# Twelve gate tiles as six pairs of seven half-size products, in a one-core hybrid decoder step

## The chip, the cores and the metric

The kernel runs on one NeuronCore of a Trainium2 chip. The metric is device time of one launch in microseconds (us), median of the runs. TensorE multiplies (PE in the profile, PEld for its weight loads), VectorE (DVE), ScalarE (ACT) and GpSimd (POOL) do elementwise work, SyncE (SP) issues most of the DMAs, ACT's queue issues the weight loads.

## The reference, cut to what matters

One layer for 1024 prompt tokens and 8 sample tokens (1032 columns in all), width 1024, float32.

```python
h = rmsnorm(x, norm_g)
proj = h @ w_in                      # 1024 -> 7688 columns
(aq, ak, av, abeta, aalpha, agate, bu, bv, bgate, cq, cgate, mg) = split(proj)
ya = delta_branch(...)               # 4 heads: conv, SiLU, gated delta rule in chunks
yb = chunk_mlp_branch(bu, bv, bgate) # LayerNorm, causal 128x128 mixing per group
yc = memory_branch(cq, cgate, k, v)  # attention to 256 memory tokens
gates = sigmoid(mg + b_gate)         # 3 x 1024 columns of proj: 24 tiles of 128
merged = gates[0]*(ya @ w_br_a) + gates[1]*(yb @ w_br_b) + gates[2]*(yc @ w_br_c)
y = rmsnorm(x + merged @ w_out, final_norm_g)
```

The changed part computes half of `mg`: twelve of its 24 feature tiles.

## The kernel before, in words

Everything is kept transposed: features on partitions, tokens along the free dimension. `hTh` and `hTl` hold h, split into a high part (fp32r) and the rest, as 8 k-tiles of 128 x 1032. A weight tile of 128 output features is split the same way into `whi` and `wlo`. `mm3` makes one product as three passes (high x high, high x low, low x high) over the 8 k-tiles: 24 matmuls. A job ("k", "v", "q", "ag", "bv", "bg", "bu", "gate", "cq", "cg") is one weight tile: `project` runs `h_group` for NS = 3 token groups of NW = 344, so 72 matmuls on line L275, into the PSUM tag `pj` (2 buffers). Other PSUM tags are `tp` (2) and `dl` (4).

The program is written as one main stream of such jobs, with side streams (Python generators) mixed in by hand. `mm3` calls `tick()` after every sixth matmul; each side stream then issues its next piece; a piece that yields n sits out n ticks. No scheduler reorders anything: each engine takes its instructions in the order in which they were issued. `run.until(cond)` ticks without main matmuls between, until the condition holds.

The main stream has these parts:

- `norm_gen`: h is normed and transposed, while the first two weight tiles (k0, v0) run in four token groups of 256 or 264.
- `plan_a`: the jobs of the four delta heads, of branch B, and 8 gates (1 beside head 1, 7 at the end). The side stream `delta_all` starts after q0. For each head `delta_gen` issues transposes, `LA` (L784/L785), a way through DRAM (`ld` L795, `Lt` L799), a solve on POOL in 31 steps (`X`, L838/L844), a second way through DRAM (`ud` L850, `U` L852), three DVE transposes into `TA` and `T2` (L855 to L857), small products (L863 to L894), and a loop over 8 chunks (L902 to L920) that carries the state `S`. It ends with `ro`, `r` (L931) and the transposes of `r`. Beside it runs `sample_gen`. At the end of the plan stands `run.until(("delta", 3) in done)`.
- `plan_c`: two gates, then eight times a gate and a `kv` job (24 matmuls of 256 columns), then for each head cq, a gate, cg, and one more gate. Side streams: `mem_norm`, `b_gen` (branch B), `att_gen` (prompt attention) and `csample_all`, which runs `csample_gen` for the heads one after another: loads of the caches, `qd` and `qb` through DRAM (L1177, L1179), two multiplies on POOL (L1184), reduction, softmax, products L1215. It ends with `run.until({("att", 3), "b"} <= done)`.
- `plan_m`: gate 0 and the 24 branch products with the merge; then the output projection.

A gate tile is copied to a `stg` buffer (3 of them), passed through a sigmoid by `gate_spill`, and stored to DRAM until `merge` needs it. `w_next` loads weights two and three jobs ahead (on ACT's queue) and splits them one job ahead (ACT L250, DVE L253).

Of the kernel before, what the change touches and what calls it, by code (L numbers as in the profile page):

```python
# [118 lines left out]
def tile_mixer_step(ctx: ExitStack, tc: tile.TileContext, a):  # L119
# [124 lines left out]
    def w_split(i, slow=True, eng=V):  # L244
        if i < len(order) and i not in splits:
# [4 lines left out]
            S.copy(out=hi, in_=raws[i])  # L250
# [2 lines left out]
            eng.tensor_tensor(out=lo, in0=raws[i], in1=f32(hi), op=ALU.subtract)  # L253
# [18 lines left out]
    def mm3(out, wh, wl, rh, rl, nk, ticks=True):  # L272
        ops = [(w(k), r(k)) for w, r in ((wh, rh), (wh, rl), (wl, rh)) for k in range(nk)]
        for i, (w, r) in enumerate(ops):
            PE.matmul(out, lhsT=w, rhs=r, start=(i == 0), stop=(i == len(ops) - 1))  # L275
# [80 lines left out]
    xst = ExitStack()
    xp = scoped(xst, "xp")
    scT = xp.tile([P, 12, 24], F32, name="scT")
    wab = xp.tile([P, KT, 8], F32, name="wab")
# [593 lines left out]

    def gate_tile(i, t):
        br, f = gate_col[i]
        b = c_bg + br * 8 + f
        project("gate", i, lambda n, sl, o: S.copy(out=t[:, sl], in_=o))  # L957
        return dict(out=t, in_=t, func=AF.Sigmoid, bias=colv[:, b:b + 1])

    def gate_spill(i, t, act):  # L960
        yield 2
        S.activation(**act)
        gate_d[i] = dr.tile([P, NT], F32, name=f"gate{i}")
        SP.dma_start(out=gate_d[i], in_=t)
# [545 lines left out]
```

## Time and profile before

| | |
|---|---|
| Runs | 1150.77, 1152.01, 1152.36 us; median 1152.01 |
| Profiled execution | span 1148.6 us, granted TensorE clock 0.995 |
| Share of the span with work | PE 97%, PEld 94%, DVE 53%, ACT 36%, POOL 19% |
| DMA | 133.5 MB, 116 GB/s mean |
| Chain that ended last | PE 90%, of which line L275 into `pj` 56% and into `dl` 20% |

The span is the time from the first to the last instruction; the median of the runs lies 3.4 us above it. PE has work all the time but for the start. What matters in such a program is whether PE's next instruction has what it needs when its turn comes; the idle time of the other engines does not count by itself.

### The profile page before, as it was taken

The page shows a single profiled execution, that of the slowest core. Times are in us where ns is not written, and L with a number is a line of the kernel's source. Part 1 is how long each engine was busy: PE and PEld are TensorE (multiplying, and loading weights), DVE is VectorE, ACT ScalarE, POOL GpSimd, SP SyncE. Part 2 cuts the span into 40 slices and gives each one's busy share as a digit, 9 for nine tenths or more (in the row PEclk, how much of TensorE's full clock was granted, in tenths as well). Part 3 has the DMA queues.
Part 4 walks back from the last instruction along what each step waited for, and adds up shares of the span by engine and source line. Part 5 has one row for each costly group of instructions (what it writes and reads, how often), then busy time and mean ns, then how long its engine had stood idle before and what let it go on. Part 6 is the DMA issues. An engine that isn't in the chain of part 4 may idle for free.

```text
span 1148.6 us, 19257 instructions
## 1 busy us (share of the span) xinstructions
PE 1119.7 (97%) x7609; PEld 1074.8 (94%) x7609; DVE 609.7 (53%) x1512; ACT 411.9 (36%) x891; POOL 214.1 (19%) x392
## 2 busy tenths in 40 slices
PE   5999999999999999999999999999999999999997
PEld 4989999999999999999999999989999999998884
DVE  6754654655465546513277432655545246786554
ACT  5434233333331333333344333545445321232232
POOL 1060715070507050600034000101101000000000
PEclk9999999999999999999999999999999999999999
DMA  8104420341143114422654556543432465662221
GB/s 250 39 20 97 132 63 23 117 129 46 40 125 104 45 41 126 124 79 77 200 138 137 166 170 186 159 118 93 146 114 74 145 195 176 212 213 100 83 93 57
DMA packets 153772, 133.53 MB, mean 116 GB/s; under 512 B 20941, under 2 KB 134922, under 8 KB 153674
## 3 DMA queue, kind: packets, MB, share of 16 engines
q1 hardware_dynamic: 72242, 89.82, 24.5%
q10 hardware_dynamic: 81440, 42.49, 13.7%
q8 instruction: 60, 0.98, 0.3%
q14 instruction: 30, 0.25, 0.1%
HBM read 100.74 MB, written 31.64 MB: 115 GB/s over the span
## 4 chain that ended last, share of the span: by engine, by line
PE 90%; DVE 4%; DMA 2%; ACT 2%; issue 1%; SPq 1%; ACTq 0%; DVEq 0%
PE pj L275 56%; PE dl L275 20%; PE tp L191 2%; PE dl L191 2%; PE dl L784 1%; DMA raw<-w_in 1%; DMA stg<-ya 1%; PE dl L894 1%; PE tp L1094 1%; PE dl L918 1%; PE dl L909 1%; PE dl L902 1%; PE dl L904 1%; PE dl L917 1%; DVE wlo L253 1%
## 5 line engine op out<-in xcount | busy, mean ns | idle before, releaser
L275 PE MATMUL pj<-hTh,whi 128*128 128x344 f32 (+1 forms) x1456 | 280.7, 327 | 3.1 <-DVE ql L155 1.1
L275 PE MATMUL pj<-hTh,wlo 128*128 128x344 f32 (+1 forms) x1456 | 277.5, 325 | 0.0
L275 PE MATMUL pj<-hTl,whi 128*128 128x344 f32 (+1 forms) x1456 | 272.3, 322 | 0.0
L275 PEld LDWEIGHTS pj<-hTh,whi 128*128 128x128 f32 x1456 | 232.4, 190 | 5.9 <-ACT hTh L393 1.5
L275 PEld LDWEIGHTS pj<-hTh,wlo 128*128 128x128 f32 x1456 | 235.1, 189 | 1.4 <-issue 0.8
L275 PEld LDWEIGHTS pj<-hTl,whi 128*128 128x128 f32 x1456 | 234.3, 188 | 1.1 <-DVE hTl L394 0.2
L253 DVE TENSOR_TENSOR wlo<-raw,whi 128x1024 fp32r<-128x1024 f32 (+1 forms) x91 | 102.5, 1126 | 51.7 <-ACT whi L250 44.2
L250 ACT CAST whi<-raw 128x1024 fp32r<-128x1024 f32 (+1 forms) x92 | 86.2, 937 | 81.5 <-PE dl L275 64.8
L957 ACT COPY stg<-pj 128x344 f32<-128x344 f32 x72 | 32.1, 446 | 108.0 <-PE pj L275 107.6
L838 POOL TENSOR_TENSOR itmp<-X,Lt 128x60 f32<-128x60 f32 (+24 forms) x124 | 43.7, 352 | 125.7 <-DMA Lt<-ld 116.5
L1184 POOL TENSOR_TENSOR kvt<-kvt,qb 128x1024 f32<-128x1024 f32 x8 | 19.2, 2419 | 210.7 <-DMA qb<-qd 130.9
L275 PE MATMUL dl<-yh,whi 128*128 128x344 f32 x288 | 57.3, 321 | 0.0
L275 PE MATMUL dl<-yh,wlo 128*128 128x344 f32 x288 | 57.3, 321 | 0.0
L275 PE MATMUL dl<-yl,whi 128*128 128x344 f32 x288 | 57.1, 320 | 0.0
L275 PEld LDWEIGHTS dl<-yh,whi 128*128 128x128 f32 x288 | 47.8, 188 | 0.0
L275 PEld LDWEIGHTS dl<-yh,wlo 128*128 128x128 f32 x288 | 47.7, 188 | 0.0
L275 PEld LDWEIGHTS dl<-yl,whi 128*128 128x128 f32 x288 | 47.6, 188 | 0.0
L844 POOL TENSOR_TENSOR X<-X,itmp 128x60 f32<-128x60 f32 (+24 forms) x124 | 43.7, 353 | 9.7
L531 ACT COPY xraw<-pj 128x344 f32<-128x344 f32 (+2 forms) x38 | 16.3, 430 | 66.4 <-PE pj L275 63.1
L906 DVE COPY y<-dl 128x128 f32<-128x128 f32 x32 | 9.3, 291 | 55.3 <-PE dl L904 34.4
L1367 DVE TENSOR_TENSOR stg<-dl,stg 128x344 f32<-128x344 f32 x48 | 24.7, 515 | 18.1 <-PE dl L275 18.1
L503 POOL TENSOR_TENSOR kq<-kq,cvt 128x512 f32<-128x512 f32 x24 | 32.6, 1358 | 1.9
(378 smaller groups left out, 1591.9 us busy)
## 6 DMA issues: line engine op xcount, KB each, us to landing
raw<-w_in ACTq DMA_DIRECT2D x57, 512.0 KB
gate<-stg SPq DMA_DIRECT2D x23, 516.0 KB
stg<-gate SPq DMA_DIRECT2D x23, 516.0 KB
x<-x_prompt SPq DMA_DIRECT2D x8, 512.0 KB
raw<-w_mem_kv ACTq DMA_DIRECT2D x8, 512.0 KB
kvt<-cache_mem_k SPq DMA_DIRECT2D x16, 256.0 KB
kvt<-cache_mem_v SPq DMA_DIRECT2D x16, 256.0 KB
wor<-w_out SPq DMA_DIRECT2D x8, 512.0 KB
```

What stands on the lines that cost most here:

```text
L191: PE.transpose(out, in_, ident[:p, :p])
L250: S.copy(out=hi, in_=raws[i])
L253: eng.tensor_tensor(out=lo, in0=raws[i], in1=f32(hi), op=ALU.subtract)
L275: PE.matmul(out, lhsT=w, rhs=r, start=(i == 0), stop=(i == len(ops) - 1))
L503: G.tensor_tensor(out=d[:, cs], in0=d[:, cs], in1=o, op=ALU.add)
L531: S.copy(out=raw[:, 3 + sl.start:3 + sl.stop], in_=o)
L784: PE.matmul(t, lhsT=kq[:, 0, sl], rhs=kq[:, :, sl], start=True, stop=True)
L838: G.tensor_tensor(out=tm, in0=X[:, 0:m, j:j + 1].to_broadcast([P, m, n]), in1=Lt[:, j:j + 1, j + 1:32].to_broadcast([P, m, n]), op=ALU.mult,)
L844: G.tensor_tensor(out=X[:, 0:m, j + 1:32], in0=X[:, 0:m, j + 1:32], in1=tm, op=ALU.subtract)
L957: project("gate", i, lambda n, sl, o: S.copy(out=t[:, sl], in_=o))
L1184: G.tensor_tensor(out=kts[hb], in0=kts[hb], in1=qb[:, hb * 4:hb * 4 + 4].unsqueeze(2).to_broadcast([P, 4, 2, P]), op=ALU.mult,)
L1367: V.tensor_tensor(out=sg[:, sl], in0=o, in1=sg[:, sl], op=ALU.mult)
```

## The change

Gates 1 to 5 run first (1 and 2 while h is being normed, in the place of k0 and v0). Then gates 6 to 17 run in six pairs by Strassen's method in Winograd's form. For two weight tiles (two block rows) and h cut in two halves of 4 k-tiles and two halves of HT = 516 tokens, seven half products replace eight: each has 4 k-tiles, three passes and two column halves of QT = 258, so 24 matmuls, 168 for a pair. Sums of h blocks (`t_hl`, made by `t_gen`) and of weight blocks (`sf`, made on POOL by `pair_sums`) are operands; the results are added from PSUM by DVE. After that come the jobs of `plan_a` without any gates, and `plan_c` with 6 gates in place of 15. From the end of the pairs on, `tick()` is called after every fourth matmul (`run.every = 4`), and a yield of n sits out n * 6 / 4 ticks, rounded up. A bare yield still waits for one tick.

```diff
 class Streams:
...
     def __init__(self):
         self.items = []
+        self.every = 6
...
-                it[1] = next(it[0]) or 0
+                it[1] = -(-(next(it[0]) or 0) * 6 // self.every)
...
-    plan_a = [
-        [("k", 0), ("v", 0), ("q", 0), ("ag", 0), ("bv", 0), ("bv", 1), ("bv", 2)],
-        [("k", 1), ("v", 1), ("q", 1), ("ag", 1), ("bv", 3), ("bg", 0), ("bu", 0)] + gates(1),
-        [("k", 2), ("v", 2), ("q", 2), ("ag", 2), ("bg", 1), ("bu", 1), ("bg", 2), ("bu", 2)],
-        [("k", 3), ("v", 3), ("q", 3), ("ag", 3), ("bg", 3), ("bu", 3)] + gates(7),
-    ]
+    plan_0 = gates(5)
+    plan_s = gates(12)
+    plan_a = []
+    for h in range(H):
+        plan_a += [("k", h), ("v", h), ("q", h), ("ag", h)]
+        plan_a += ([("bv", 0), ("bv", 1), ("bv", 2)], [("bv", 3), ("bg", 0), ("bu", 0)],
+                   [("bg", 1), ("bu", 1), ("bg", 2), ("bu", 2)], [("bg", 3), ("bu", 3)])[h]
     plan_c = gates(2)
-    for j in range(8):
-        plan_c += gates(1) + [("kv", j)]
+    for j in range(0, 8, 2):
+        plan_c += [("kv", j), ("kv", j + 1)] + (gates(1) if j < 6 else [])
     n_kv = len(plan_c)
     for h in range(H):
-        plan_c += [("cq", h)] + gates(1) + [("cg", h)]
+        plan_c += [("cq", h), ("cg", h)]
     plan_c += gates(1)
...
-            if ticks and i % 6 == 5:
+            if ticks and i % run.every == run.every - 1:
                 tick()
...
+    def t_gen():
...
+        def minus(o, x, y, lo):
+            V.tensor_tensor(out=o, in0=f32(x[0]), in1=f32(y[0]), op=ALU.subtract)
+            G.tensor_tensor(out=lo, in0=f32(x[1]), in1=f32(y[1]), op=ALU.subtract)
...
+        f1, d, f2 = new(), new(), new()
+        minus(f1, h_blk(1, 2), h_blk(1, 1), d)
+        yield 5
+        V.tensor_tensor(out=f1, in0=f1, in1=d, op=ALU.add)
...
+        f3, d = new(), new()
+        minus(f3, h_blk(2, 2), h_blk(1, 2), d)
+        V.tensor_tensor(out=t_hl[4][1], in0=f4, in1=f32(t_hl[4][0]), op=ALU.subtract)
+        yield 5
+        V.tensor_tensor(out=f3, in0=f3, in1=d, op=ALU.add)
+        yield 2
+        S.copy(out=t_hl[3][0], in_=f3)
+        yield 2
+        V.tensor_tensor(out=t_hl[3][1], in0=f3, in1=f32(t_hl[3][0]), op=ALU.subtract)
+        done.add("tsum")
...
+    run.add(t_gen())
+    for _, i in plan_0[2:]:
+        t = stage()
+        run.add(gate_spill(i, t, gate_tile(i, t)))
+    run.until(lambda: "tsum" in done)
...
+    def product(banks, n, x, first):
+        wh, wl = wt[n]
+        for q in range(2):
+            ts = slice(q * QT, (q + 1) * QT)
+            ops = [(w, r, k) for w, r in ((wh, x[0]), (wh, x[1]), (wl, x[0])) for k in range(HK)]
+            for i, (w, r, k) in enumerate(ops):
+                PE.matmul(
+                    banks[q], lhsT=w[:, k], rhs=r[:, k, ts], start=(first and i == 0), stop=(i == len(ops) - 1),
+                    skip_group_check=True,
+                )
+                if i % run.every == run.every - 1:
+                    tick()
...
+    def pair_job(p, i, j):
...
+        pair_split(p, ("a12", 3))
+        b_a = bank(pj)
+        product(b_a, "a11", h_blk(1, 1), True)
+        for q in range(2):
+            S.copy(out=p1[:, qs[q]], in_=b_a[q])
+        pair_split(p, (4,))
+        b_b = bank(dl)
+        product(b_b, 2, t_hl[2], True)
+        plus(u2, b_b, p1)
...
+        product(b_b, 3, t_hl[3], False)
+        plus(u3, b_b, p1)
+        pair_sums(p + 2, (3, 4))
...
+        product(b_c, 4, h_blk(2, 2), False)
+        plus(ti[:, HT:], b_c, u2)
+        run.add(pair_store(i, j, ti, tj))
...
+    run.every = 4
...
+    for kind in ("k", "v", "q"):
+        project(kind, 0, qkv_tile(kind, 0))
```

Three places show what moves. On PE at the end of delta head 3, before (L275 is the main stream, L909 to L918 the last chunk, `ident,r` the last transposes of the head):

```order
L275 MATMUL pj<-hTh,wlo 128x344 x6
L909 MATMUL dl<-y,kd 128x128
L917 MATMUL dl<-S,gcb 128x128
L918 MATMUL dl<-y,LA 128x128
L275 MATMUL pj<-hTh,whi 128x344 x8
L275 MATMUL pj<-hTl,whi 128x344 x8
L275 MATMUL pj<-hTh,wlo 128x344 x8
L275 MATMUL pj<-hTh,whi 128x344 x8
L275 MATMUL pj<-hTl,whi 128x344 x4
L191 MATMUL dl<-ident,r 128x128 x4
```

Main matmuls stand between the steps of the head. After (the main stream is now L280, the same steps are L1121 to L1130, and `ident,r` ends the head):

```order
L1121 MATMUL dl<-y,kd 128x128
L1129 MATMUL dl<-S,gcb 128x128
L1130 MATMUL dl<-y,LA 128x128
L1114 MATMUL dl<-r,U 128x128
L1116 MATMUL dl<-S,Kg 128x128
L1121 MATMUL dl<-y,kd 128x128
L1129 MATMUL dl<-S,gcb 128x128
L1130 MATMUL dl<-y,LA 128x128
L195 MATMUL dl<-ident,r 128x128 x8
L280 MATMUL pj<-hTh,whi 128x344 x8
```

None stands there any more. The stretch without them begins on PE where the last job of `plan_a` ends (`kqn,st` to `dd` are `sample_gen`'s, L1075 and L1076 the first small products after `TA` and `T2`):

```order
L280 MATMUL pj<-hTh,wlo 128x344 x4
L195 MATMUL dl<-ident,kq 128x128 x4
L280 MATMUL pj<-hTh,wlo 128x344 x4
L898 MATMUL tp<-kqn,st 128x2 x8
L912 MATMUL tp<-do_7069,ones 128x8
L195 MATMUL tp<-ident,dd 8x128
L1075 MATMUL dl<-TA,LA 32x32
L1076 MATMUL dl<-T_7207,LA 32x32
```

From the last `LA` product of head 3 (L996, before L784) to L1075 there are 44 main matmuls now, for the other heads 240, before 294 for each. On PE at the end of `plan_c`, before (`pb`, `pTs` and `so` are steps of `csample_gen` for head 3):

```order
L191 MATMUL tp<-ident,pb 128x8 x2
L275 MATMUL pj<-hTh,whi 128x344 x6
L191 MATMUL tp<-ident,p 128x128 x2
L275 MATMUL pj<-hTh,whi 128x344 x2
L275 MATMUL pj<-hTl,whi 128x344 x8
L275 MATMUL pj<-hTh,wlo 128x344 x2
L1215 MATMUL tp<-kvt,pTs 32x128 x8
L275 MATMUL pj<-hTh,wlo 128x344 x6
L1215 MATMUL tp<-kvt,pTs 32x128 x8
```

After (the first three rows of L195 and L1415 are still head 2's, from `qsm` on it is head 3):

```order
L195 MATMUL tp<-ident,pb 128x8 x2
L1415 MATMUL tp<-kvt,pTs 32x128 x16
L195 MATMUL tp<-ident,so 128x128 x2
L195 MATMUL tp<-ident,qsm 8x128
L195 MATMUL tp<-ident,sc 8x128 x2
L195 MATMUL tp<-ident,pb 128x8 x2
L1415 MATMUL tp<-kvt,pTs 32x128 x16
L195 MATMUL tp<-ident,so 128x128 x2
L280 MATMUL pj<-hTh,whi 128x344 x8
```

The whole sample attention of head 3 now stands behind the last job of the plan, with nothing between its steps.

More of the change, by code (lines that the diff above doesn't have):

```diff
@@ L29 @@
 NS = 3
+HK = KT // 2
+HT = NT // 2
+QT = HT // 2
 H = 4
@@ L233, in w_of @@
         return w_in_v[:, :, c:c + P], KT
-    order = [(k, i) + w_of(k, i) for k, i in sum(plan_a, []) + plan_c + plan_m]
+    order = [(k, i) + w_of(k, i) for k, i in plan_0 + plan_s + plan_a + plan_c + plan_m]
+    in_pair = range(len(plan_0), len(plan_0) + len(plan_s))
     raws, splits, w_pos = {}, {}, [0]
@@ L244, in w_split @@
     def w_split(i, slow=True, eng=V):
-        if i < len(order) and i not in splits:
+        if i < len(order) and i not in splits and i not in in_pair:
             nk = order[i][3]
@@ L355, in tile_mixer_step @@
     SP.dma_start(out=a["sc_sample"][:, 0:2, :], in_=a["state_conv"][:, 1:3, :])
[L356 to L359, printed above, removed]
+    scT = const.tile([P, 12, 24], F32, name="scT")
+    wab2 = const.tile([P, KT, 16], F32R, name="wab2")
+    wab = np_.tile([P, KT, 8], F32, name="wab", bufs=1)
     SP.dma_start(out=wab, in_=w_in_v[:, :, O_AB:O_AB + 8])
-    wab2 = xp.tile([P, KT, 16], F32R, name="wab2")
     nss = np_.tile([P, 9], F32, name="nss", bufs=1)
@@ L399, in const_gen @@
         V.tensor_copy(out=colv, in_=t[:, :89])
+        done.add("const")
         yield
@@ L535, in qkv_tile, with gate_tile, gate_act, gate_store @@
         return evac
-    e_k, e_v = qkv_tile("k", 0), qkv_tile("v", 0)
+    def gate_tile(i, t):
+        br, f = gate_col[i]
+        b = c_bg + br * 8 + f
+        project("gate", i, lambda n, sl, o: S.copy(out=t[:, sl], in_=o))
+        return dict(out=t, in_=t, func=AF.Sigmoid, bias=colv[:, b:b + 1])
+    def gate_act(i):
+        br, f = gate_col[i]
+        b = c_bg + br * 8 + f
+        return dict(func=AF.Sigmoid, bias=colv[:, b:b + 1])
+    def gate_store(i, t):
+        gate_d[i] = dr.tile([P, NT], F32, name=f"gate{i}")
+        SP.dma_start(out=gate_d[i], in_=t)
+    def gate_spill(i, t, act):
+        yield 2
+        while "const" not in done:
+            yield
+        S.activation(**act)
+        gate_store(i, t)
     w_pos[0] = 2
     w2 = [splits.pop(0), splits.pop(1)]
+    t2 = [stage(), stage()]
     for n in range(4):
@@ L542, in tile_mixer_step @@
         sl = slice(n * 256, (n + 1) * 256 if n < 3 else NT)
-        for w, ev in zip(w2, (e_k, e_v)):
-            ev(NS - 1 if n == 3 else 0, *h_group(w, n, sl))
+        for w, t in zip(w2, t2):
+            _, o = h_group(w, n, sl)
+            S.copy(out=t[:, sl], in_=o)
             if n == 3:
@@ L547, in tile_mixer_step, with h_blk @@
                     pass
+    for i, t in zip((1, 2), t2):
+        run.add(gate_spill(i, t, dict(out=t, in_=t, **gate_act(i))))
+    run.until(lambda: "const" in done)
     nst.close()
-    project("q", 0, qkv_tile("q", 0))
+    sst = ExitStack()
+    tpl = scoped(sst, "tsum", side="right")
+    t_hl = {n: [tpl.tile([P, HK, HT], F32R, name=f"t{n}{x}") for x in "hl"] for n in (2, 3, 1, 4)}
+    def h_blk(i, j):
+        ks, ts = slice((i - 1) * HK, i * HK), slice((j - 1) * HT, j * HT)
+        return hTh[:, ks, ts], hTl[:, ks, ts]
@@ new lines, in tile_mixer_step, with pair_sums @@
+    run.add(t_gen())
[3 more added lines that the diff above has]
+    run.until(lambda: "tsum" in done)
+    tst.close()
+    spool = scoped(sst, "pair")
+    sf, s4, wt = {}, {}, {}
+    def pair_sums(p, which):
+        if p not in pairs:
+            return
+        a1, a2 = raws[p], raws[p + 1]
+        for n in which:
+            sf[n] = spool.tile([P, HK, P], F32, tag=f"sf{n}", name=f"sf{n}")
+            x, y, op = {
+                1: lambda: (a2[:, :HK], a2[:, HK:], ALU.add),
+                2: lambda: (sf[1], a1[:, :HK], ALU.subtract),
+                3: lambda: (a1[:, :HK], a2[:, :HK], ALU.subtract),
+                4: lambda: (a1[:, HK:], sf[2], ALU.subtract),
+            }[n]()
+            G.tensor_tensor(out=sf[n], in0=x, in1=y, op=op)
@@ new lines, in pair_split @@
+    def pair_split(p, names):
+        if p not in pairs:
+            return
+        a1, a2 = raws[p], raws[p + 1]
+        src = {"a11": a1[:, :HK], "a12": a1[:, HK:], "a22": a2[:, HK:]}
+        if len(names) == 1:
+            hi = spool.tile([P, HK, P], F32R, tag="s4h", name="s4h")
+            lo = spool.tile([P, HK, P], F32R, tag="s4l", name="s4l")
+        else:
+            hi = wp.tile([P, KT, P], F32R, tag="whi", name="whi")
+            lo = wp.tile([P, KT, P], F32R, tag="wlo", name="wlo")
+        for q, n in enumerate(names):
+            x = src[n] if n in src else sf[n]
+            h, l = hi[:, q * HK:(q + 1) * HK], lo[:, q * HK:(q + 1) * HK]
+            S.copy(out=h, in_=x)
+            V.tensor_tensor(out=l, in0=x, in1=f32(h), op=ALU.subtract)
+            wt[n] = (h, l)
@@ L551, in tile_mixer_step @@
+    pairs = list(in_pair)[::2]
+    w_load(pairs[0])
+    w_load(pairs[0] + 1)
+    pair_sums(pairs[0], (1, 2, 3, 4))
+    w_load(pairs[0] + 2)
+    w_load(pairs[0] + 3)
+    pair_split(pairs[0], ("a11", 2))
+    for p in pairs:
+        pair_job(p, order[p][1], order[p + 1][1])
+    w_pos[0] = pairs[-1] + 2
+    sst.close()
+    run.every = 4
+    xst = ExitStack()
+    xp = scoped(xst, "xp")
+    for kind in ("k", "v", "q"):
+        project(kind, 0, qkv_tile(kind, 0))
     dp = scoped(dst, "dp")
@@ L952, in delta_all @@
             yield from delta_gen(h)
[L954 to L964, printed above, removed]
     ug_t = {}
@@ L991, in tile_mixer_step @@
     run.add(delta_all())
-    for kind, i in sum(plan_a, [])[3:]:
+    for kind, i in plan_a[3:]:
         job(kind, i)
```

57 lines of the change are left out of this document (added).

## The prediction

> **What bounds the kernel now.** I read the page's busy shares first, then the busy time by stretch, and the timeline where the change moves something. The first row is the page's on PE; the second is a stretch with a delta head beside the main stream: us from and to, length, then PE, PEld, DVE, ACT and POOL busy with counts, granted clock, DMA share and GB/s.
>
> ```profile
> PE 1119.7 (97%) x7609; PEld 1074.8 (94%) x7609; DVE 609.7 (53%) x1512; ACT 411.9 (36%) x891; POOL 214.1 (19%) x392
> 165.00:279.00 114.00, 113.57 (x837) 111.15 (x837) 62.15 (x168) 40.13 (x104) 38.26 (x85) 1.00 0.29 84
> ```
>
> PE is covered even there. So time is the sum of PE's work, and two things can change it: what a matmul costs, and whether PE must now wait for a side stream.
>
> **The products.** Start-to-start distances of matmul groups give the price. These are PE rows: start, length, line, shapes, count.
>
> ```profile
> 30.88 1.11 PE L275 MATMUL pj<-hTh,whi 128*128 128x256 f32 x8
> 31.83 0.65 PE L275 MATMUL pj<-hTl,whi 128*128 128x256 f32 x4
> ...
> 684.25 1.44 PE L275 MATMUL pj<-hTl,whi 128*128 128x344 f32 x8
> 685.52 1.44 PE L275 MATMUL pj<-hTh,wlo 128*128 128x344 f32 x8
> 686.80 1.07 PE L275 MATMUL pj<-memTh,whi 128*128 128x256 f32 x8
> 687.71 1.07 PE L275 MATMUL pj<-memTl,whi 128*128 128x256 f32 x8
> ```
>
> A 344-column matmul takes 1.27/8 = 158.8 ns, one of 256 takes 0.95/8 = 118.8 on h and 0.91/8 = 113.8 on the memory tokens. For 258 I take 119.0, since most operands are h (119.7 if it grows with the columns). A pair cost 144 x 158.8 = 22.86 us and will cost 168 x 119.0 = 19.99: over six pairs -17.2 us (-22.5 at 113.8, -16.5 at 119.7).
>
> Here a rule of the Trainium skill speaks against the change: "Perfetto Trace Analysis", section "Identifying the Most-Contended Engine", counts weight-load busy time as the good measure for TensorE, and PEld stands at 94%. By that rule 24 more weight loads in a pair would cost, not save: 26.7 us a pair at 158.8 ns each, 1264 in all. The trace does not bear it out: the 256-column rows have a weight load for each matmul too and run at 118.8 ns, so I keep -17.2.
>
> Beside the products a pair loads ACT, DVE and POOL with casts, subtractions, sums and evictions of half tiles. By these groups of the page (128 x 1024: 937 ns on ACT, 1126 on DVE, 2419 on POOL) that is under 9 us on each engine in 20 us, and each result is wanted one product (2.9 us) or more after it can start. I cost it at nothing; if that cover were gone, a late split would cost up to 2 us per pair. The twelve stores on SP's queue and the weight loads on ACT's (1 MB each way per 20 us) have the room that the gates had before.
>
> ```profile
> L253 DVE TENSOR_TENSOR wlo<-raw,whi 128x1024 fp32r<-128x1024 f32 (+1 forms) x91 | 102.5, 1126 | 51.7 <-ACT whi L250 44.2
> L250 ACT CAST whi<-raw 128x1024 fp32r<-128x1024 f32 (+1 forms) x92 | 86.2, 937 | 81.5 <-PE dl L275 64.8
> ...
> L1184 POOL TENSOR_TENSOR kvt<-kvt,qb 128x1024 f32<-128x1024 f32 x8 | 19.2, 2419 | 210.7 <-DMA qb<-qd 130.9 <-DMA kvt<-cache_mem_v 79.7
> ```
>
> **Entry into the pairs.** `t_gen` needs 44 ticks and the three gates beside it give 36, so its end is issued without products: f3 = f3 + d, cast, subtraction. Its operands have 2064 columns: 2.3 us on DVE, 1.9 on ACT, 4.9 on POOL. The last POOL subtraction is issued at tick 32 (30.4 us after the gates' start, at 6 x 158.8 ns a tick) and ends at 35.3; DVE's add ends 37.6, ACT's cast 39.5, and only then can ACT cast a11 for the first product, whose low part waits for DVE until about 42.5. The gates end at 34.3. PE waits about 7.5 us (4 if POOL is quicker, 12 if DVE and POOL hinder each other).
>
> **Delta heads 0 to 2.** A bare yield is four matmuls now. Between the last `LA` product and the first small product (L863) of a head 240 matmuls stand instead of 294. The chain in that time goes `LA`, `ld`, `Lt`, POOL, `ud`, `U`, three DVE transposes. Its rows, each from an answer of its own (the first three head 1's, the others head 3's; for a line the last two times are the first and last start):
>
> ```profile
> L784 PE MATMUL dl<-kq x16: 377/379/379, 214.9 to 221.0; 128*128 128x256 f32 x16
> 263.07 2.61 SPq L852 DMA_DIRECT2D U<-ud  x4
> 267.06 0.43 DVE L857 STREAM_TRANSPOSE TA<-U 32x256 f32<-32x256 f32 x1
> L784 PE MATMUL dl<-kq x64: 377/379/483, 101.3 to 449.5; 128*128 128x256 f32 x64
> 457.86 0.24 POOL L838 TENSOR_TENSOR itmp<-X,Lt 128x31 f32<-128x31 f32 x1 [28.98 <-DMA Lt<-ld]
> 483.93 2.52 SPq L850 DMA_DIRECT2D ud<-X  x4
> 487.99 1.95 SPq L852 DMA_DIRECT2D U<-ud  x4
> 500.39 0.21 PE L863 MATMUL dl<-TA,LA 32*32 32x32 f32 x1
> ```
>
> Head 3 had 500.4 - 449.5 = 50.9 us; less 294 x 158.8 ns that leaves 4.2 for side work on PE. Now it is 38.1 + 4.2 = 42.3. Head 1's chain took 267.5 - 221.0 = 46.5 us, head 3's, with the same 4.4 from `U`'s issue to the last transpose, 492.4 - 449.5 = 42.9. DVE takes its work in order, so the next job's `wlo` is stuck behind a late transpose, and PE behind both. I take 4.2 for head 1 and the middle, 2.4, for heads 0 and 2: +9 us (0 if DMAs are quicker without the gates' stores, 15 if each has 5 us).
>
> **The tail of head 3.** PE's order has 44 main matmuls after `LA`: 7.0 us, with side work 8.6. Then PE has only this head. Counted from 449.5 in the rows above: POOL starts at 8.4 and ends at 34.4; `U` is issued at 38.5 and DVE done at 42.9. Up to the loop come five rounds of small products that depend on each other through ACT and DVE; with 0.6 to 1.6 us for a round of products and 0.4 to 0.8 for what follows it, as in the timeline after 500.39, I estimate 7.7 us. In the loop the dependences are these (PE's rows, then DVE's):
>
> ```profile
> 518.51 0.39 PE L904 MATMUL dl<-S,Kg 128*128 128x128 f32 x2
> 518.65 1.20 PE L275 MATMUL pj<-hTh,wlo 128*128 128x344 f32 x6
> 519.69 0.38 PE L909 MATMUL dl<-y,kd 128*128 128x128 f32 x2
> ...
> 520.27 1.18 PE L275 MATMUL pj<-hTh,whi 128*128 128x344 f32 x6
> ...
> 538.16 0.39 PE L918 MATMUL dl<-y,LA 128*128 128x128 f32 x2
> 518.93 0.29 DVE L906 COPY y<-dl 128x128 f32<-128x128 f32 x1 [1.33 <-PE dl L904]
> 520.11 0.35 DVE L912 SCALAR_TENSOR_TENSOR S<-S,egl,dl 128x128 f32<-128x128 f32 x1 [0.89 <-PE dl L909]
> ...
> 541.77 1.23 DVE L931 TENSOR_TENSOR r<-r,ro 128x1024 f32<-128x1024 f32 x1
> ```
>
> L904 to `y` 0.42, `y` 0.29, L909 to `S` 0.42, `S` 0.35, and two hand-overs of 0.06: 1.6 us a chunk, 12.8 for eight. From the last L918 to the end of L931 it is 4.8, the transposes make it 5.6. Sum 42.9 + 7.7 + 12.8 + 5.6 = 69.0, so PE is held for 60.4 us. In it lie the head's own products, which took PE time before as well: 0.58 for three of a chunk's five (519.69 to 520.27), so 0.95 for all, 7.6 for eight chunks, and about as much for the rest. Net +45 us (38 if POOL is quicker with DVE quiet, 53 if the loop is slower).
>
> **Memory keys.** `mem_norm` has two gates beside it instead of three, and six ticks are left over. Before, its input came late already (us in all, times, longest):
>
> ```profile
> ACT xn L302 <- DMA x<-mem_prompt: 6.9, 2, 4.7
> ```
>
> ACT waited and PE was covered by evictions two deep. With one gate less, transposes and splits of two half tiles are open to PE: +2 us as an estimate (0, as before; 6, about the wait shown).
>
> **The tail of sample attention.** When the last gate of `plan_c` ends, 61 ticks are left over, before 1: the end of head 2 (about 3.5 us until `qd` can be issued) and all of head 3. The rows are head 3's before, from SP's, POOL's and DVE's timelines:
>
> ```profile
> 855.11 0.30 SPq L1177 DMA_DIRECT2D qd<-qrow  x1
> 858.09 0.33 SPq L1179 DMA_DIRECT2D qb<-qd  x1
> 862.37 4.79 POOL L1184 TENSOR_TENSOR kvt<-kvt,qb 128x1024 f32<-128x1024 f32 x2 [39.12 <-DMA kvt<-cache_mem_v]
> 872.12 1.22 DVE L1189 TENSOR_REDUCE sc<-kvt 128x8 f32<-128x1024 f32 x1
> ```
>
> After the 3.5: 3.0 to `qb`, 4.3 until POOL starts, 4.8 on POOL, 1.2 for the second reduction, and an estimated 5.5 for softmax, transposes and products: 22.3 us, less some 4 of products that PE had before. +18 (12 if the first and last part are half as long, 25 if cache loads, which must wait for buffers, come late).
>
> **The clock.** The granted clock after a wait is seen at the start (us, PE busy, clock, DMA):
>
> ```profile
> 22.00:24.00 2.00, 2.00 (x11) 0.50 0.52 129
> 24.00:26.00 2.00, 2.00 (x18) 0.96 0.47 65
> ```
>
> Eleven records fit where eighteen fit two us later: I take 1.6 us lost for each restart. Three long waits cost 5 us so, and small products in the tail, PE nearly idle around them, about 3 more: +8 (0 to 12). "TensorE: Matmul & The Clock Gate", section "What's actually happening", in the Trainium skill says that an idle window of about 3.4 us puts the clock back to half; the start agrees, and no row shows it in the middle of the kernel. With an unaffected clock the sum would be 8 lower, 1216.
>
> At no cost: constants moved to another pool, k0 and v0 now as ordinary jobs, gates 1 and 2 in their place; the start is covered as before.
>
> **Sum.** -17.2 + 7.5 + 9 + 45 + 2 + 18 + 8 = +72.3 on the span of 1148.6: 1220.9. The median of the runs lies 3.4 above that span, so 1224. All low ends together give +31.5 (1183), all high ends +106.5 (1259).
>
> **Rivals.**
> - Not slower: PE takes the next job's matmuls while a side stream's product waits. Then tails and entry cost nothing and 1152 - 17 = 1135 is left; it decides as soon as less than 17 us of waits remain. For it speaks only that PE is busy 97%. Against it stands this row, where PE idled 1.04 us with independent h products next in its order. Chance 0.03.
>
> ```profile
> 445.12 1.13 PE L784 MATMUL dl<-kq 128*128 128x256 f32 x4 [1.04 <-DVE LA L785]
> ```
>
> - Weight loads bind: each of the 168 matmuls costs what one of the 144 costs now. Then a pair takes 168 x 158.8 ns, six are +22.9 instead of -17.2, and the time is 1264. For it speaks PEld's 94%, against it the 256-column rows. Chance 0.03. (The page named at the products would have it so.)
> - Heads 0 to 2 lose much more, some 10 us each, because conversions, splits and transposes crowd on DVE in less time: +21 on the forecast, 1245. DVE was at 62 of 114 us in 165 to 279, and 240 matmuls instead of 294 bring it to two thirds, so it has room. Chance 0.10.
> - My forecast 0.83; the rest, 0.01, is no change: tails and saving cancel.
>
> About 0.2% is what a measurement of this kernel can tell. Faster 0.03, same 0.01, slower 0.96. The range 1190 to 1256 leaves out the first two rivals and the outer corners of the unknown terms.
>
> **What would show it.** Right: PE idle for some 45 us in one stretch before gate 18's first product, with POOL's solve in it, and some 18 before gate 0's; half clock after both; L681 matmuls 119 ns apart; PE waiting for DVE at L1075 in heads 0 to 2. Wrong: main products between the steps of head 3's loop in time, or L681 at 150 ns or more.

## The result, and the profile after

The changed kernel takes 1287.79 us (median of 4 runs, 1287.09 to 1289.77), the kernel before 1152.18 us beside it: ratio 1.1177, 95% interval 1.116 to 1.1194. That is 135.6 us more; the forecast was 72 more. The sign was right, the size was not.

These are two rows of the page of the kernel after: PE, and the granted TensorE clock in 40 slices.

```profile
PE 1148.7 (89%) x7753; PEld 1090.0 (85%) x7753; DVE 692.1 (54%) x1612; ACT 423.4 (33%) x911; POOL 266.1 (21%) x420
PEclk9989999988999998999995899999999699999999
```

PE's busy time rose by 29 us although the products got cheaper; slices with a granted clock of 5 or 6 tenths, of which the kernel before had none in its middle, are part of that. The rest is waiting. PE's waits after (what PE waited to do, on which result, us in all, times, longest):

```profile
PE dl L1075 <- DVE TA L1067: 23.2, 1, 23.2
PE dl L195 <- DVE r L1143: 20.8, 4, 7.1
PE tp L195 <- DVE sc L1389: 17.2, 1, 17.2
...
PE dl L280 <- ACT pth L158: 9.4, 4, 3.3
PE pj L681 <- ACT whi L671: 6.0, 1, 6.0
PE dl L996 <- DVE LA L997: 5.1, 4, 1.8
PE tp L912 <- DVE do L909: 4.3, 3, 2.9
```

Rows 1, 3 and 5 are the two tails and the entry into the pairs, all forecast. Row 2 was not, but for the 4.6 us of it that lie inside head 3's tail: `r` is the end of a delta head, and heads 0 to 2 are waited for too. Nor was the row on `pth`, attention beside the main stream.

To see where the 138.1 us between the two spans lie, I cut both traces at the first product of each job and took off the job's products at their undisturbed price (158.8 ns for 344 columns, 118.8 for 256, 226.6 for 512; a pair at the 20.17 us that the later pairs take). What is left over is side work and waiting on PE:

| Stretch | before | after | difference |
|---|---|---|---|
| to the end of the gates ahead of the pairs | 12.1 | 18.2 | +6.1 |
| pair 0 over the other five | | 3.0 | +3.0 |
| delta heads, until the end of head 3 | 111.8 | 198.2 | +86.3 |
| memory keys and values, to kv 7 | 16.9 | 29.2 | +12.4 |
| cq 0 to gate 23 | 41.9 | 85.8 | +43.9 |
| gate 0 to the end | 10.4 | 13.6 | +3.2 |

With -16.2 for the products and -0.5 for an earlier start the sum is 138.2.

### The profile page after: what moved, and what is told of

Read it like the earlier page. It is cut to its first block, busy times and chain, and to the rows that moved or that the text cites. A ratio compares the mean times of both kernels' runs of the same rounds, so it can differ in the third digit from the quotient of the medians.

```text
span 1286.7 us, 19746 instructions
## 1 busy us (share of the span) xinstructions
PE 1148.7 (89%) x7753; PEld 1090.0 (85%) x7753; DVE 692.1 (54%) x1612; ACT 423.4 (33%) x911; POOL 266.1 (21%) x420
## 4 chain that ended last, share of the span: by engine, by line
PE 71%; DVE 10%; DMA 6%; issue 4%; POOL 4%; ACT 4%; SPq 1%; POOLq 0%; ACTq 0%; DVEq 0%
PE pj L280 31%; PE dl L280 19%; PE dl L681 7%; PE pj L681 2%; POOL itmp L1050 2%; PE dl L195 2%; POOL X L1056 1%; PE tp L195 1%; PE dl L996 1%; DMA bt<-bv 1%; DVE rs_t L168 1%; DVE wlo L258 1%; PE dl L1121 1%; PE dl L1106 1%; DVE rs_t L169 1%
## 5 line engine op out<-in xcount | busy, mean ns | idle before, releaser
L280 PE MATMUL pj<-hTh,whi 128*128 128x344 f32 (+2 forms) x1168 | 231.4, 335 | 1.8 <-ACT stg L543 1.1
L280 PE MATMUL pj<-hTh,wlo 128*128 128x344 f32 (+2 forms) x1168 | 221.6, 328 | 0.0
L280 PE MATMUL pj<-hTl,whi 128*128 128x344 f32 (+2 forms) x1168 | 221.0, 328 | 0.0
L280 PEld LDWEIGHTS pj<-hTh,whi 128*128 128x128 f32 x1168 | 193.2, 197 | 4.0 <-ACT stg L543 1.4
L280 PEld LDWEIGHTS pj<-hTl,whi 128*128 128x128 f32 x1168 | 191.3, 193 | 0.7 <-issue 0.4
L280 PEld LDWEIGHTS pj<-hTh,wlo 128*128 128x128 f32 x1168 | 190.0, 192 | 1.8 <-issue 0.2
L258 DVE TENSOR_TENSOR wlo<-raw,whi 128x1024 fp32r<-128x1024 f32 (+1 forms) x79 | 89.6, 1135 | 54.5 <-ACT whi L255 54.1
L1384 POOL TENSOR_TENSOR kvt<-kvt,qb 128x1024 f32<-128x1024 f32 x8 | 20.9, 2633 | 187.9 <-DMA kvt<-cache_mem_v 102.3
L280 PE MATMUL dl<-yh,whi 128*128 128x344 f32 x288 | 57.4, 321 | 0.0
L280 PE MATMUL dl<-yh,wlo 128*128 128x344 f32 x288 | 57.3, 321 | 0.0
L280 PE MATMUL dl<-yl,whi 128*128 128x344 f32 x288 | 57.1, 320 | 0.0
L280 PEld LDWEIGHTS dl<-yh,whi 128*128 128x128 f32 x288 | 47.8, 188 | 0.0
L280 PEld LDWEIGHTS dl<-yl,whi 128*128 128x128 f32 x288 | 47.7, 188 | 0.0
L280 PEld LDWEIGHTS dl<-yh,wlo 128*128 128x128 f32 x288 | 47.6, 188 | 0.0
L534 ACT COPY xraw<-pj 128x344 f32<-128x344 f32 x36 | 16.1, 447 | 72.3 <-PE pj L280 72.1
L506 POOL TENSOR_TENSOR kq<-kq,cvt 128x512 f32<-128x512 f32 x24 | 33.6, 1402 | 1.9
L280 PE MATMUL dl<-woh,mh 128*128 128x512 f32 x128 | 32.5, 396 | 0.0
L1349 ACT ACTIVATE p<-dl,mx 128x256 f32<-128x256 f32 x32 | 15.2, 475 | 52.4 <-DVE mx L1344 52.2
```

Of the source, the lines that this page charges most:

```text
L506: G.tensor_tensor(out=d[:, cs], in0=d[:, cs], in1=o, op=ALU.add)
L534: S.copy(out=raw[:, 3 + sl.start:3 + sl.stop], in_=o)
L1349: S.activation(out=p, in_=s, func=AF.Exp, bias=mx, scale=DKS, accum_out=su)
L1384: G.tensor_tensor(out=kts[hb], in0=kts[hb], in1=qb[:, hb * 4:hb * 4 + 4].unsqueeze(2).to_broadcast([P, 4, 2, P]), op=ALU.mult,)
```

## Experiments

Two theories are tested. **Spacing**: the side chains are mixed in by hand, so what counts is how many main products stand between a result and its use; ticks after every fourth matmul leave too few, and PE waits inside every head. **Cover**: the waits come because the gates are gone that stood beside the chains, whatever the ticks. Each ratio is against the kernel before, run beside it (1149.9 to 1150.9 us).

**The changed kernel with ticks as before (a_every6).**

```diff
-    run.every = 4
+    run.every = 6
```

> The changed kernel with run.every = 6 kept to the end; all else as changed. Theory S (spacing: ticks after every fourth matmul leave the side chains too little time, and PE waits for them in every head and in the attention part): the time above the bare products between k0 and bg3 falls from 127 us to about 95, that of cq0 to cg3 from 52 to about 36, the tail of head 3 stays (92 ticks left over instead of 87), the tail of the sample attention gets a little shorter (49 instead of 61): 1225 to 1240 us. Theory C (cover: the waits come because the gates are gone, whatever the ticks): the heads lose as before, the tails get longer: 1285 to 1300 us.

1245.42 us, ratio 1.0818 (1.0793 to 1.0842): 42 us of the loss go with one number, some 5 less than the least that theory S asked for. Heads 0, 1 and 2 have 23.1, 22.1 and 24.2 us over their products, as before the change (23.3, 24.8, 23.7) and against 32.7, 36.1 and 37.8 after it. The stretches of heads 1 and 2, `k1` to `k3`, first of the kernel after, then of this one (us from and to, length, PE, PEld, DVE, ACT, POOL busy with counts, clock, DMA share, GB/s):

```profile
327.00:572.00 245.00, 226.01 (x1631) 218.77 (x1631) 136.37 (x338) 73.62 (x200) 84.65 (x191) 0.97 0.28 76
```

```profile
317.00:535.00 218.00, 217.74 (x1616) 213.58 (x1615) 117.25 (x301) 72.47 (x199) 74.53 (x151) 1.00 0.29 81
```

The same jobs take 245 and 218 us; PE has hardly a gap left and the clock stays full. The tails do not get shorter, though. From the last product of `bu3` to the first of gate 18 pass 84.6 us with wide ticks and 64.4 with close ones, while the ticks left over there are nearly the same (92 and 87): with wide ticks no main product stands between head 3's last `LA` product and L1075, with close ones 44 do. So head 3's stretch is 10.6 us longer, against 37.2 that heads 0 to 2 gain. The second tail, from the last product of gate 23 to the first of gate 0, takes 30.4 us with wide ticks and 28.8 with close ones, though 49 ticks are left over there instead of 61. The number of ticks left over does not tell the time of a tail.

**The kernel before with close ticks (b_every4).**

```diff
     def __init__(self):
         self.items = []
+        self.every = 6
...
-                it[1] = next(it[0]) or 0
+                it[1] = -(-(next(it[0]) or 0) * 6 // self.every)
...
-            if ticks and i % 6 == 5:
+            if ticks and i % run.every == run.every - 1:
...
+    run.every = 4
     project("q", 0, qkv_tile("q", 0))
```

> The kernel before, with every = 4 (and yields scaled likewise) from q0 on: no gate moved, no Strassen, nothing left over at the two ends. Theory S: heads 0 to 2 lose about 10 us each and head 3 as much, the attention part 10 to 20: 1190 to 1210 us, with PE waiting for r at the end of each head. Theory C: 1148 to 1160 us.

1188.85 us, ratio 1.0332 (1.0306 to 1.0357), with no gate moved: spacing by itself costs 38 us. Of these 31.6 lie in the four heads, 3.4 in keys and values, 2.8 from cq 0 to gate 23; the last is less than I had expected. The two changes nearly add up: +94.5 us for the moved gates and the pairs with wide ticks (a_every6), +37.9 for close ticks in the kernel before, 132.4 together; the changed kernel has +135.6. PE's waits in this kernel:

```profile
PE dl L192 <- DVE r L933: 11.3, 3, 7.0
PE dl L786 <- DVE LA L787: 4.5, 4, 1.2
PE tp L192 <- DVE ptl L156: 2.3, 4, 1.3
PE tp L634 <- DVE gp L630: 2.1, 1, 2.1
PE dl L866 <- DVE T L858: 2.0, 1, 2.0
```

From the last product of a head's loop to the transposes of `r` 36 main products stand before, 5.7 us, and the chain in between takes 4.5 to 5.5: no wait. With close ticks 28 products stand there, 4.4 us, and the chain takes 6.6 us in heads 1 and 2 and 11.6 in head 0. The margin was one microsecond wide. Why the chain is longer now, DVE and POOL show (start, length, line, shapes):

```profile
191.47 1.04 DVE L165 TENSOR_TENSOR rs_t<-ro 128x8 f32<-128x8 f32 x1
192.55 0.96 DVE L166 SCALAR_TENSOR_TENSOR rs_t<-rs_t,ms 128x8 f32<-128x8 f32 x1
193.54 0.17 DVE L167 SCALAR_TENSOR_TENSOR ro<-rs_t,ro 128x8 f32<-128x8 f32 x1
193.74 1.15 DVE L165 TENSOR_TENSOR rs_t<-ro 128x8 f32<-128x8 f32 x1
194.92 0.96 DVE L166 SCALAR_TENSOR_TENSOR rs_t<-rs_t,ms 128x8 f32<-128x8 f32 x1
...
197.15 1.08 DVE L507 TENSOR_SCALAR kq<-scT,colv 128x8 f32<-128x8 f32 x1
...
198.33 1.23 DVE L167 SCALAR_TENSOR_TENSOR ro<-rs_t,ro 128x8 f32<-128x8 f32 x1
```

```profile
191.45 1.04 POOL L502 TENSOR_TENSOR kq<-xraw,colv 128x512 f32<-128x512 f32 x1 [6.07 <-ACT xraw L532]
192.45 1.04 POOL L502 TENSOR_TENSOR cvt<-xraw,colv 128x512 f32<-128x512 f32 x1
193.56 1.30 POOL L504 TENSOR_TENSOR kq<-kq,cvt 128x512 f32<-128x512 f32 x1
194.82 1.04 POOL L502 TENSOR_TENSOR cvt<-xraw,colv 128x512 f32<-128x512 f32 x1
```

The steps on DVE have eight columns. Of the nine steps of the reciprocal root six take 0.96 to 1.23 us, the others 0.15 to 0.17. The slow ones end where an instruction of POOL ends (the rows show it for the first four): POOL runs the convolution of the next head's q. The faster ticks have pushed the end of one head onto the next one's convolution.

**Room ahead of `r` (b4_rroom), no convolution on POOL (b4_convdve), both (b4_both).** All three on the kernel before with close ticks.

```diff
         while ("ag", h) not in done:
             yield
-        yield 2
+        yield 8
         for half in range(2):
```

```diff
-        if key[0] == "q":
-            tmp = xp.tile([P, T], F32, tag="cvt", name="cvt", bufs=1)
...
-        else:
-            V.tensor_scalar(out=d, in0=raw[:, 0:T], scalar1=cw[0], scalar2=None, op0=ALU.mult)
+        V.tensor_scalar(out=d, in0=raw[:, 0:T], scalar1=cw[0], scalar2=None, op0=ALU.mult)
...
-            if key[0] != "q":
-                V.scalar_tensor_tensor(out=d, in0=raw[:, j:j + T], scalar=cw[j], in1=d, op0=ALU.mult, op1=ALU.add)
+            V.scalar_tensor_tensor(out=d, in0=raw[:, j:j + T], scalar=cw[j], in1=d, op0=ALU.mult, op1=ALU.add)
```

> The kernel before with every = 4 (1188.9 us), and ahead of the transposes of r a yield of 8 instead of 2 (12 ticks instead of 3). If the price of close ticks lies at the places where a chain has too few ticks (PE waited 11.3 us for r in three heads, and ran at a low clock behind each), this one edit takes 11 to 17 us: 1172 to 1178. If the time is lost anyway and the wait only moves to the next step: 1185 to 1190.

> The kernel before with every = 4 (1188.9 us), and the convolution of q on DVE like that of k and v, none on POOL. In the wait of 7.0 us for r nine steps of the reciprocal root on DVE took about 1 us each instead of 0.17 while POOL ran the convolution of the next q. Theory P (POOL's work slows those steps): the long wait shrinks to some 2 us as in the heads where POOL is quiet there, 1181 to 1186. Rival (the steps are slow for another reason, or the added DVE work costs as much): the wait of 7 stays or moves, 1188 to 1196.

> The kernel before with every = 4, with both edits (12 ticks ahead of the transposes of r, convolution of q on DVE). If they act on two different losses: 1188.9 - 15.7 - 15.5 = 1158. If both only take away the one long wait for r and what follows it (the heads then keep the short waits for LA, and the attention part its 6 us): 1165 to 1172.

1173.20 us (ratio 1.0204, 1.0186 to 1.0222), 1173.40 (1.0201, 1.0179 to 1.0224) and 1168.02 (1.0162, 1.0145 to 1.0179). The first is as expected in time; but a low clock stood only behind the first of the three waits for `r`, and behind the other two, of 2.2 us each, it stayed at 1.00. The second gains 15.5 us, nearly twice the most that theory P gave it. The waits for `r` account for 7.9 of them (11.3 to 3.4); the rest is not taken apart. Its DVE rows for the same steps, with POOL quiet:

```profile
186.97 0.17 DVE L165 TENSOR_TENSOR rs_t<-ro 128x8 f32<-128x8 f32 x1
187.17 0.17 DVE L166 SCALAR_TENSOR_TENSOR rs_t<-rs_t,ms 128x8 f32<-128x8 f32 x1
187.37 0.17 DVE L167 SCALAR_TENSOR_TENSOR ro<-rs_t,ro 128x8 f32<-128x8 f32 x1
187.57 0.17 DVE L165 TENSOR_TENSOR rs_t<-ro 128x8 f32<-128x8 f32 x1
```

0.17 us each instead of up to 1.23. The chain to `r` takes 5.1 us instead of 11.6 in head 0, and the longest wait for `r` is 1.4 instead of 7.0. That POOL's convolution slows these steps is shown. Both edits together take 20.8 us, not 31: they remove largely the same wait, as the second case of the expectation had it. What stays, 17.6 us over the kernel before, is spread: by the stretches about 3 us in each head, 2 in keys and values, 4.5 from cq 0 to gate 23.

**Both edits in the changed kernel (a4_both).** The same two diffs, on the changed kernel.

> The changed kernel with both edits and nothing else (96 ticks left over at the end of the first plan instead of 87). If the loss in the heads is the price of close ticks as in the kernel before: 1287.8 less 18 to 25, plus some 3 for the longer tail: 1265 to 1273. If want of cover makes part of it: above 1278.

1262.13 us, ratio 1.0968 (1.0951 to 1.0984). That is 3 us below the range of the first case. Heads 0 to 2 fall from 32.7, 36.1 and 37.8 us to 28.2, 29.2 and 28.3: 20.9 of the 34.8 us that they had lost. In the kernel before with close ticks the two edits take 17.7 of 27.2 in the same heads. So the larger part of the heads' loss is the same in both kernels; the 13.9 us that stay here are not taken apart.

**Cover for the tails (a_p3_tail6, a_p3_c6, a6_p3_tail6).** Three pairs instead of six; the six gates go behind `bu3`, or into `plan_c`, or behind `bu3` with `run.every = 6`.

```diff
-    plan_s = gates(12)
+    plan_s = gates(6)
...
-                   [("bg", 1), ("bu", 1), ("bg", 2), ("bu", 2)], [("bg", 3), ("bu", 3)])[h]
+                   [("bg", 1), ("bu", 1), ("bg", 2), ("bu", 2)], [("bg", 3), ("bu", 3)] + gates(6 if h == 3 else 0))[h]
```

```diff
-    plan_s = gates(12)
+    plan_s = gates(6)
...
-        plan_c += [("cq", h), ("cg", h)]
-    plan_c += gates(1)
+        plan_c += [("cq", h)] + gates(1) + [("cg", h)]
+    plan_c += gates(3)
```

> The changed kernel with three pairs instead of six; the six gates that this frees stand as ordinary jobs at the end of the first plan, beside delta head 3 (0 ticks left over there instead of 87). The tail of head 3 cost 54 us net by the stages; half of the products' saving, 8.1 us, is given back: 1288 - 54 + 8 = 1242. Theory C: 1238 to 1245. Theory S: head 3 keeps some 10 us of waits like the other heads: 1247 to 1255. If the tail was not for want of cover: above 1275.

> The changed kernel (every = 4) with three pairs instead of six, and six gates back in the second plan: one between cq and cg of each head and two more at its end (0 ticks left over there instead of 61). If the loss of 43.9 us from cq0 to gate 23 is for want of cover, it falls to 3 to 5 as in the kernel before with every = 4: 1287.8 - 40 + 8 = 1256 us (1250 to 1260). If spacing makes the attention's waits for pth, only the tail goes: 1264 to 1270.

> The changed kernel with run.every = 6, three pairs instead of six, and six gates at the end of the first plan (20 ticks left over there instead of 92). If spacing and cover add up: 1245.4 - 46 for the covered tail + 8 for the products given back = 1207 us (1200 to 1215). If more cover and wide ticks don't add up, since one chain sets the length either way: 1225 to 1240.

1247.74 us (ratio 1.0839, 1.0817 to 1.0861), 1256.73 (1.0933, 1.0915 to 1.095) and 1208.54 (1.0497, 1.0465 to 1.0528). In the first, the delta stretch falls from 198.2 to 150.5 us over its products: the tail of head 3 was worth 47.7 net. 38.6 stay above the 111.8 of before, with no tail left, and the time lies in the range of theory S. Of these, close ticks alone cost 31.6 in the kernel before; no run separates the other 7. The waits for `r` stay too:

```profile
PE dl L195 <- DVE r L1143: 16.3, 3, 7.1
```

In the second, cq 0 to the last gate falls from 85.8 to 45.1, the value of the kernel before with close ticks (44.7). So nearly all of the attention's loss was want of cover. The third shows that the two causes add up: with wide ticks the delta stretch has 120.8. Heads 0 to 2 are then at 68.9 (before the change 71.8), and 18.0 us of tail are left behind the last gate of the plan.

**The pairs by themselves (a_plain12).** The twelve gates as ordinary jobs in the place of the pairs:

```diff
-    for _, i in plan_0[2:]:
+    for _, i in plan_0[2:] + plan_s:
         t = stage()
         run.add(gate_spill(i, t, gate_tile(i, t)))
```

(`t_gen`, the pairs and their pools are left out.)

> The changed kernel with its twelve early gates as ordinary jobs of 72 products instead of the six pairs, and no sums of h blocks. Both theories: the products cost 12 x 11.43 = 137.2 us instead of 6 x 20.17 + 3.0 = 124.0, and the wait of 6.2 us ahead of the pairs goes: 7 us more than the changed kernel, 1295 us (1291 to 1299). If the pairs disturb what comes after them, under 1288.

1292.64 us, ratio 1.1231 (1.1205 to 1.1257). By the two ratios the pairs with their entry gain 6 us; by the stretches 13.2 - 6.2 = 7.0. Without any pair the kernel is still 12% slower than the one before: it is the moved gates and the ticks that cost, not Strassen's products. Rows of a later pair of the changed kernel show the price of a product:

```profile
121.81 0.65 PE L681 MATMUL dl<-t3h,whi 128*128 128x258 f32 x4
122.29 0.64 PE L681 MATMUL dl<-t3l,whi 128*128 128x258 f32 x4
...
123.72 0.65 PE L681 MATMUL dl<-t3l,whi 128*128 128x258 f32 x4
124.20 0.65 PE L681 MATMUL dl<-t3h,wlo 128*128 128x258 f32 x4
```

Twenty products start in 2.39 us, 119.5 ns apart. A pair from the second on takes 20.17 us in all (120.1 ns a product), against 22.87 for two gates.

**A warm clock at the entry (a_warm).**

```diff
+    o = pj()[:, :NW]
+    for i in range(36):
+        PE.matmul(o, lhsT=hTh[:, 0, :P], rhs=hTh[:, i % KT, :NW], start=(i == 0), stop=(i == 35))
     for p in pairs:
         pair_job(p, order[p][1], order[p + 1][1])
```

> The changed kernel with 36 products of 344 columns, whose result nothing uses, ahead of the first pair, where PE waited 6.0 us. They fit into the wait (36 x 158.8 ns = 5.7 us). If the 3.0 us that the first pair took over the others are the price of a low clock behind the wait, pair 0 takes 20.2 us like the rest and the kernel 3 us less: 1284 to 1286. If pair 0 is late for another reason (its splits, the sums of weight blocks), nothing changes, or the wait moves behind the 36: 1287 to 1289.

The first theory misses. The clock did stay full:

```profile
88.00:90.00 2.00, 1.70 (x11) 1.41 (x11) 0.66 (x1) 1.83 (x2) 0.00 (x0) 1.00 0.76 188
90.00:92.00 2.00, 1.11 (x8) 0.90 (x8) 2.00 (x2) 0.00 (x0) 0.27 (x1) 1.00 0.25 74
92.00:94.00 2.00, 1.69 (x14) 1.70 (x15) 0.25 (x1) 0.00 (x0) 1.92 (x2) 1.00 0.00 0
```

In the changed kernel the same time has 0.50:

```profile
86.00:88.00 2.00, 0.00 (x0) 0.00 (x0) 1.50 (x1) 0.47 (x1) 0.00 (x0) 0.88 0.66 264
88.00:90.00 2.00, 0.00 (x0) 0.00 (x0) 0.52 (x1) 1.96 (x2) 0.00 (x0) 0.50 0.63 150
90.00:92.00 2.00, 1.99 (x8) 1.79 (x8) 2.00 (x2) 0.00 (x0) 0.14 (x1) 0.50 0.38 113
92.00:94.00 2.00, 1.66 (x8) 1.56 (x8) 0.39 (x1) 0.00 (x0) 1.92 (x2) 0.50 0.00 0
```

But pair 0 takes 23.12 us all the same. Where the slow clock had stretched the products, PE now waits, by its timeline:

```profile
92.31 0.76 PE L681 MATMUL pj<-hTh,wlo 128*128 128x258 f32 x4 [1.20 <-DVE wlo L672]
...
95.45 0.77 PE L681 MATMUL dl<-t2h,whi 128*128 128x258 f32 x4 [0.94 <-ACT whi L671]
```

Pair 0's 3.0 us belong to the splits of its weights, in a line behind the last sums. The run took 1281.66 us, ratio 1.1155 (1.1138 to 1.1173), an interval that meets that of the changed kernel. The entry and pair 0 take what they took (18.1 us instead of 18.2, and 23.12 both times); most of the difference lies in the delta heads (193.4 us over their products instead of 198.2), where nothing was edited, so I claim no gain.

**The best I could make of it (s_best).** Both edits; `plan_0 = gates(6)`, `plan_s = gates(6)`; the jobs in this order:

```diff
+    k0 v0 q0 ag0 bv0 bv1 k1 v1 q1 ag1 bv2 bv3 bg0 k2 v2 q2 ag2 bu0 bg1 bu1 k3 v3 q3 ag3 bg2 bu2 bg3 bu3 gate gate gate
+    gate gate kv0 ... kv7 cq0 gate cg0 cq1 gate cg1 cq2 gate cg2 cq3 gate cg3 gate gate
```

> The changed kernel with both edits, four gates beside the sums of h blocks, three pairs, the jobs k, v, q of a head moved up so that the next head starts when the last ends, three gates behind bu3, and eight gates in the second plan (two ahead of kv0, one between cq and cg of each head, two at the end): 6 ticks left over at the first end, none at the second. If every tail and the entry go with their leftovers, the pairs' 8.1 us remain against the price of close ticks (6 in the attention part, 5 to 10 in the heads, some for the thinner kv part): 1152 to 1162, about the kernel before. If moving k, v, q up makes new waits: 1170 and more.

1208.57 us, ratio 1.0508 (1.0491 to 1.0525): a miss. Both tails are gone and the entry with pair 0 costs 1.5 instead of 9.1, but the denser heads have 148.2 us over their products (before: 111.8) and cq 0 to the last gate 60.9 (41.9). New waits show it:

```profile
PE dl L981 <- DVE LA L982: 11.5, 4, 4.8
PE tp L195 <- DVE ptl L159: 5.9, 6, 2.9
PE pj L277 <- DVE wlo L255: 5.7, 6, 1.7
```

The same side work beside fewer jobs waits in new places. No version with pairs came near the kernel before: the best two stand at 1208.5. The kernel before has 0 ticks left over at the first end and 1 at the second, so it has no gate to spare: a gate in a pair saves 2.70 / 2 = 1.35 us, while a gate beside a chain can hide up to its own length, 11.4.

## Why the prediction was right and wrong

On the spans the sum said +72.3 and the runs +138.1. Of the 66 us between, 26 lie in delta heads 0 to 2, 26 in the stretch of the attention and 10 in keys and values.

- **Products**, -17.2 forecast: -16.2 (6 x 2.70). The trace bears out the row of 256 columns, not that of weight loads which bind: the time of the kernel, 1288, is above the 1264 of that rival, but the pairs are no part of its cause.
- **Entry**, +7.5: 6.0 of waiting, +6.1 by the stretches. Three more in pair 0, which I had priced at nothing: its splits are late too.
- **Delta heads 0 to 2**, +9 and at most +15: the step that failed. They measure +34.8 (9.4, 11.3 and 14.1). With head 3's own share (I had priced that head by its tail alone) it is +38.6 in the kernel with a covered tail, and +31.6 from close ticks alone. I had counted main products for one chain, from `LA` to `TA`, where 240 instead of 294 mattered little: PE's wait at L1075 in heads 0 to 2 does not show. The sentence "A bare yield is four matmuls now" holds for all chains, and the short ones had a margin of one microsecond. My rival of 10 us a head had the right size, but for the wrong reason and at a chance of 0.10; DVE was not short of time (136 of 245 us in heads 1 and 2), its small steps waited for POOL.
- **Tail of head 3**, +45: +47.7. The total is close, its parts less so. From the last `LA` product PE comes to L1075 after 39.8 us (42.9 counted), the small products up to the loop take 13.0 (7.7), the loop 14.2 (12.8), the end 6.5 (5.6): 73.4 instead of 69.0. PE during the solve, from L1075 to the end of the head, and at the start of gate 18:

```profile
675.00:698.00 23.00, 0.35 (x2) 0.04 (x2) 6.57 (x22) 0.26 (x1) 13.67 (x45) 0.50 0.19 54
698.00:732.00 34.00, 22.78 (x211) 20.14 (x212) 11.55 (x38) 8.12 (x31) 0.00 (x0) 0.75 0.08 20
...
732.00:734.00 2.00, 2.00 (x9) 2.00 (x8) 1.90 (x3) 0.00 (x0) 0.00 (x0) 0.50 0.00 0
734.00:736.00 2.00, 2.00 (x9) 2.00 (x8) 0.53 (x1) 0.00 (x0) 0.00 (x0) 0.50 0.89 287
736.00:738.00 2.00, 2.00 (x15) 2.00 (x14) 0.00 (x0) 0.00 (x0) 0.00 (x0) 0.99 0.83 270
```

- **Memory keys**, +2 and at most +6: +12.4 with close ticks, +2.5 with wide ones. The gates alone cost what I said; I had not put the tick spacing on this stretch. Close ticks alone cost 3.4 there, so 6.5 come only with both; why is not shown.
- **Tail of sample attention**, +18 and at most +25: the second step that failed, +43.9 from cq 0 to gate 23. What stands behind the last job is +27 (gate 23's stretch 33.6 instead of 6.3), just above my range. But I read only that. The gates between cq and cg also covered the prompt attention, and their loss I had put at nothing: +16.6 from cq 0 to cg 3, nearly all of which goes when they come back.
- **Clock**, +8: right in kind, too small. Behind the tail of head 3 PE ran 4 us at 0.50; there gate 18's products start 287 ns apart instead of 158.8, and about 1.8 us are lost at that restart (1.6 forecast). At the entry it cost nothing by itself. But the shorter waits, which I had not foreseen, bring restarts of their own: in the middle of the kernel the clock stands at 0.50 in 16 stretches, where the kernel before has one (75.4 to 78.8). By the distances of their starts I estimate that main products lose some 13 us in them, before 1.5; these lie inside the other terms. That "the start agrees" with an idle window of 3.4 us was a misreading: the longest wait close ahead of the half clock there is 2.4 us (it ended at 19.45). And the kernel before has a row at half clock in its middle (last section).

Of the signs I had named, idle PE ahead of gate 18 and gate 0, half clock behind both and products of 119 ns came; waits at L1075 in heads 0 to 2 did not.

## What to carry to other kernels

In a program whose streams are mixed by hand, a job that is made cheaper or moved is also the cover of what stands beside it: count, for each chain and not for the longest alone, the products that stand between result and use, and compare them with the chain's time. A change of the tick rate is a change of all these distances; try it alone, in the old kernel, before it rides with another change. And look at what a moved chain now runs beside: two engines may share more than the order shows.

## What the hardware showed that I had not expected

- Instructions of eight columns on DVE took 0.96 to 1.23 us instead of 0.17 while POOL worked through 512 columns, and ended with POOL's. With the same work moved off POOL they took 0.17 again. "SBUF — State Buffer" in the Trainium skill, section "Who interferes with whom", says that a DVE instruction with two inputs in SBUF contends with a GpSimd instruction that reads SBUF, and calls this contention an exclusive lock. The rows of L165 and L166 agree; the one of 0.17 among them began between two of POOL's. The row of L507, one input beside a column of scalars, took 1.08 too, which that sentence does not tell.
- How long PE must wait before the clock falls did not come out as one number. In the changed kernel PE stood still from 84 us, and the clock fell about 3.5 us later (0.88 in 86 to 88, then 0.50). But a wait of 1.9 us, from 812.2, was enough for 3.4 us at half clock:

```profile
812.00:814.00 2.00, 0.24 (x3) 0.04 (x1) 1.97 (x3) 0.15 (x1) 0.00 (x0) 1.00 0.74 160
814.00:816.00 2.00, 1.84 (x9) 1.80 (x10) 0.71 (x2) 0.00 (x0) 0.00 (x0) 0.64 0.96 341
816.00:818.00 2.00, 2.00 (x11) 2.00 (x10) 1.97 (x3) 0.21 (x1) 0.00 (x0) 0.51 0.47 165
```

In the kernel before with close ticks waits of 1.1 us (ended at 230.7) and 2.2 us (ended at 317.3) left it at 1.00:

```profile
230.00:232.00 2.00, 1.31 (x7) 1.16 (x8) 1.60 (x5) 1.68 (x2) 0.00 (x0) 1.00 0.34 128
...
317.00:319.00 2.00, 1.73 (x14) 1.72 (x15) 0.96 (x2) 0.00 (x0) 0.00 (x0) 1.00 0.00 0
```

And the kernel before was at half clock from 75.4 to 78.8 without any wait of PE there, behind small products (L583 to L595, which use 16 rows or 16 columns of the array instead of 128):

```profile
76.00:78.00 2.00, 2.00 (x9) 2.00 (x8) 1.97 (x3) 0.51 (x3) 1.92 (x3) 0.50 0.00 0
```

"TensorE: Matmul & The Clock Gate" in the Trainium skill, section "What's actually happening", puts the clock back to half after an idle window of about 3.4 us. The wait from 84 us fits that; the one of 1.9 us and the row at 76 do not, so in this kernel shorter waits cost clock too. What besides the length of a wait decides is not shown.
